# A hybrid decoder layer: dilated and MLA head pairs in turn, and six buffers for the copied-out value columns

## The chip, the cores and the metric

The kernel runs on one core of a Trainium2 chip, as one launch. The metric is the device time of that launch in microseconds, the median of the runs. TensorE (PE) does matrix products and transposes; its weight loads are listed apart (PEld). VectorE (DVE), ScalarE (ACT) and GpSimd (POOL) do elementwise work, and SyncE (SP) issues every DMA of this kernel from one queue that is worked off in order.

## The reference, cut to what matters

One causal decoder layer over 1024 tokens of width 1024, in float32. A combined input projection gives the latents of eight multi-head-latent (MLA) heads and the queries, keys and values of eight dilated heads. The two head groups are independent of each other; both results go into one output projection, then a gated feed-forward part with a short causal convolution follows.

```python
h = rms_norm(x, g_mix_norm[l]) * (1.0 + sc1[:, None]) + sh1[:, None]
proj = h @ w_in[l]
q_lat, kv_lat, k_pe, qd, kd, vd = jnp.split(proj, SPLITS, axis=-1)
...
o_mla = causal_dense_attention(q_mla, k_mla, v_mla, (MLA_NOPE + MLA_ROPE) ** -0.5)
...
o_dil = dilated_attention(qd, kd, vd)
mix = jnp.concatenate([o_mla.reshape(B, S, MLA_HEADS * MLA_V),
                       o_dil.reshape(B, S, DIL_WIDTH)], axis=-1) @ w_o[l]
x = x + g1[:, None] * mix
```

The dilated attention is a weighted sum of three banded softmaxes; the kernel computes it as one masked softmax whose mask holds the logarithm of how many bands a key lies in.

## The kernel before, in words

Every float32 product is made of float32r parts: an operand is split into a rounded part (`hi`, copied by ACT) and a rest (`lo`, subtracted by DVE or POOL), and two or three products are accumulated in PSUM.

The work comes in stages. First the input projection: after the latents, a loop over `u` in (0, 1) takes 256 columns each of the dilated queries, the dilated keys (both through `rope_chunk`, L350) and the dilated values (L466 to L471). Each of these makes eight token tiles `p` of 24 products on PE. The query and key tiles pass ACT, DVE and POOL (norm and rotation) and are written to DRAM (`qd_s`, `kd_s`, L369). A value tile is only copied from PSUM by ACT into `vo` (L470) and written to `vd_s` (L471). Four PSUM banks hold `p`. Between the chunks `ada_late` works off columns of `w_ada` on DVE; these weights and those of the projections share three `raw` buffers.

Then the latents are transposed (L491) and split by ACT and DVE (L492, L493), and two more projections give the MLA queries, keys and values, which are written to DRAM as well. They begin with `ql_hi`, and their weights pass `split_weights` (L91 on ACT, L97 on POOL).

Then the attention, one pair of heads after another. `sources` lists the pairs: 0 to 3 are dilated, 4 to 7 MLA. `attention_loads` (L501) brings queries, keys and values of a pair from DRAM, into one buffer each (`ql_t`, `kl_t`, `vl_t`). `prepared` (L532) transposes and splits them into tiles tagged `qk`, of which there are eight. An MLA pair takes all eight: `hi` and `lo` of queries and keys for two heads. A dilated pair takes four, and then builds stacked operands by 12 DMA copies of 64 partitions by 1024 floats (L554), 0.26 MB each: `q2` and `k2` have one buffer per head, and the two `k3` are the fifth and sixth `qk` tile. A score of a dilated pair is two products over 128 rows, that of an MLA pair three over 96. Pair 0 is prepared without copies, from tiles of its own.

For a pair, `scores` (L627) runs for the first four query tiles (`hf` 0) of both heads and then for the last four (`hf` 1): products, mask and row minimum on DVE (L641), exponential on ACT (L644), normalization on POOL (L645, L646). `weighted_values` (L660) transposes the weights and multiplies them with the split values. It is called one half late: the last half of a pair comes after the first scores of the next. `prepared` for the next pair is called after the `hf` 1 scores of a pair, and the loads of the pair after that at the end of the loop body. The load of the keys of the last pair is `first_load`: the loads of the output projection's weights (L790, L791) are queued behind it on SP.

The order of the instructions on each engine is not the program's: a scheduler works it out from the program's order as priority and from its own model of the times, and gives a tile a buffer when one is free in that model. At run time each engine takes its instructions in that order.

Of the kernel before, what the change touches and what calls it, by code (L numbers as in the profile page):

```python
# [8 lines left out]
F32 = mybir.dt.float32  # L9
# [9 lines left out]
P = 128  # L19
# [22 lines left out]
def hybrid_layer(ctx, tc, x, c, positions, w_ada, b_ada, g_mix_norm, w_in, g_q_lat, w_q_b, g_kv_lat, w_kv_b,  # L42
# [183 lines left out]
    def scale_cols(gm, j, base, g0):  # L226
        V.scalar_tensor_tensor(gm[:, 2 * j:2 * j + 2], in0=modc[:, base + 2 * j:base + 2 * j + 2], scalar=1.0,
                               in1=cols[:, g0 + 2 * j:g0 + 2 * j + 2], op0=ALU.add, op1=ALU.mult)
# [30 lines left out]
    def proj_weights(c0, n):  # L259
        raw = raw_tile(KD, n)  # L260
        nc.sync.dma_start(raw, w_in[:, c0:c0 + n].rearrange("(k p) n -> p k n", p=P))
        return split_weights(raw, KD, n)
# [5 lines left out]
    def proj_mm(w, t, n):  # L268
        ps = bank("p")
        for k in range(KD):  # L270
            proj_step(ps, w, t, n, k)
        return ps
# [59 lines left out]
    ap = phA.enter_context(tc.tile_pool(name="phAw", bufs=1, reuse_waits="tile"))  # L332
# [14 lines left out]
    def ada_late(j, row_form=False):  # L347
        ada_chunk(j, ada_load(j, raw_tile(KD, 256)), row_form, True)

    def rope_chunk(c0, tabc, tabs, dst, col):  # L350
        w = proj_weights(c0, 256)
        for t in range(NT):
            ps = proj_mm(w, t, 256)
            p3 = ps[:, 0:256].rearrange("p (h d) -> p h d", d=HD)
            b3 = [P, 4, HD]
            xn = ap.tile(b3, F32, tag="xn", name="xn", bufs=4)
            A.activation(xn, p3, AF.Copy)
            sq = ap.tile(b3, F32, tag="sq", name="sq", bufs=2)
            A.activation(sq, xn, AF.Square)
            ss = ap.tile([P, 4], F32, tag="ss", name="ss", bufs=4)  # L360
            V.tensor_reduce(ss, sq, op=ALU.add, axis=AX.X)
            r = rstd_of(ap, ss, 4, 1.0 / HD, "h4")
            V.tensor_tensor(xn, xn, r[:, :, None].to_broadcast(b3), op=ALU.mult)
            o = ap.tile(b3, F32, tag="ro", name="ro", bufs=4)
            G.tensor_tensor(o, xn, tabc[:, t:t + 1, :].to_broadcast(b3), op=ALU.mult)
            b = ap.tile(b3, F32, tag="rb", name="rb", bufs=3)
            swap_mult(V, b, xn, tabs[:, t, :], 0, HD)
            V.tensor_tensor(o, o, b, op=ALU.add)
            nc.sync.dma_start(dst[t, :, col:col + 256], o)  # L369
# [89 lines left out]
    for u in range(2):  # L459
        rope_chunk(C_QD + u * 256, qc, qs, qd_s, u * 256)  # L460
        ada_late(16 + 2 * u)
        ada_late(12 + 2 * u)
        rope_chunk(C_KD + u * 256, kc, ks, kd_s, u * 256)
        ada_late(17 + 2 * u)
        ada_late(13 + 2 * u)
        w = proj_weights(C_VD + u * 256, 256)  # L466
        for t in range(NT):
            ps = proj_mm(w, t, 256)
            o = ap.tile([P, 256], F32, tag="vo", name="vo", bufs=2)
            A.activation(o, ps[:, 0:256], AF.Copy)  # L470
            nc.sync.dma_start(vd_s[t, :, u * 256:(u + 1) * 256], o)  # L471
        for j in range(2):
            scale_cols(gm2, 2 * u + j, 32, G0_FFN)
            ada_late(20 + 2 * u + j)
# [26 lines left out]
    def attention_loads(q_s, k_s, v_s, pr, wd):  # L501
        ql = bl.tile([P, NT, 2 * wd], F32, tag="ql", name="ql_t", bufs=1)
        nc.sync.dma_start(ql, q_s[:, :, pr * 2 * wd:(pr + 1) * 2 * wd].rearrange("t p c -> p t c"))
        kl = bl.tile([P, NT, 2 * wd], F32, tag="kl", name="kl_t", bufs=1)
        kins = nc.sync.dma_start(kl, k_s[:, :, pr * 2 * wd:(pr + 1) * 2 * wd].rearrange("t p c -> p t c"))
        vl = bl.tile([P, NT, P], F32, tag="vl", name="vl_t", bufs=1)
        nc.sync.dma_start(vl, v_s[:, :, pr * P:(pr + 1) * P].rearrange("t p c -> p t c"))
        return ql, kl, vl, kins.ins

    def transposed(loads, wd, hh, fused, first=False):  # L510
        tag = "x"
        gain = 1.0 if fused else kgc[0:MW, 0:1]
        rows_ = 2 * wd if fused else wd
        pair = []
        for src, tg, g in ((loads[0], "q", 1.0), (loads[1], "k", gain)):
            if first:
                hi, lo = [bl.tile([P, S], F32R, tag=f"{tg}2{u}", name=tg + "2", bufs=1) for u in range(2)]
            else:
                hi, lo = [ap.tile([P, S], F32R, tag="qk", name=tg + u, bufs=8) for u in ("hi", "lo")]
            for hf in range(2):  # L520
                ps = bank(tag)
                for i in range(4):
                    T.transpose(ps[0:rows_, i * P:(i + 1) * P], src[:, 4 * hf + i, hh * wd:hh * wd + rows_], ident)
                cs = slice(hf * 512, hf * 512 + 512)
                A.activation(hi[0:rows_, cs], ps[0:rows_, :], AF.Copy, scale=g)
                V.scalar_tensor_tensor(lo[0:rows_, cs], in0=ps[0:rows_, :], scalar=g,
                                       in1=hi[0:rows_, cs].bitcast(F32), op0=ALU.mult, op1=ALU.subtract)
            pair.append((hi, lo))
        return pair

    sources = [(qd_s, kd_s, vd_s, pr, HD) for pr in range(4)] + [(qm_s, km_s, vm_s, pr, MW) for pr in range(4)]
    def prepared(pr, loads):  # L532
        if pr >= 4:
            heads = []
            for hh in range(2):
                (qh, ql), (kh, kl) = transposed(loads, MW, hh, False)
                heads.append([(a[0:MW, :], b[0:MW, :]) for a, b in ((qh, kh), (qh, kl), (ql, kh))])
            return heads
        (qh, ql), (kh, kl) = transposed(loads, HD, 0, True, pr == 0)
        heads = []  # L540
        if pr == 0:
            for odd in range(2):
                me = slice(64 * odd, 64 * odd + 64)
                heads.append([(a[me, :], b[me, :]) for a, b in ((qh, kh), (qh, kl), (ql, kh))])
            return heads
        for odd in range(2):
            me = slice(64 * odd, 64 * odd + 64)
            other = slice(64 - 64 * odd, 128 - 64 * odd)
            q2 = bl.tile([P, S], F32R, tag=f"q2{odd}", name="q2", bufs=1)
            k2 = bl.tile([P, S], F32R, tag=f"k2{odd}", name="k2", bufs=1)  # L550
            k3 = ap.tile([P, S], F32R, tag="qk", name="k3", bufs=8)
            for dst, rows_, src in ((q2, me, qh), (q2, other, ql), (k2, me, kh), (k2, other, kh),
                                    (k3, me, kl), (k3, other, kl)):
                nc.sync.dma_start(dst[rows_, :].bitcast(F32), src[me, :].bitcast(F32))  # L554
            heads.append([(q2, k2), (q2, k3)])
        return heads

    loaded = attention_loads(qd_s, kd_s, vd_s, 0, HD)
    for u in range(2):
# [3 lines left out]
        for t in range(NT):  # L563
# [14 lines left out]
            o = mp.tile(b3, F32, tag="ro", name="rom", bufs=4)  # L578
# [11 lines left out]
    for u in range(2):  # L590
# [3 lines left out]
        for t in range(NT):  # L594
# [6 lines left out]
            vo = mp.tile([P, 4, VD], F32, tag="vo", name="vom", bufs=3)  # L601
# [7 lines left out]
            o = mp.tile([P, 4, MW], F32, tag="ro", name="rok", bufs=4)  # L609
# [13 lines left out]
    ap = phB.enter_context(tc.tile_pool(name="phB", bufs=1, reuse_waits="tile"))  # L623
# [36 lines left out]
    def weighted_values(hf, prs, vs, mrow):  # L660
# [21 lines left out]
        for odd, po in enumerate(pos):  # L682
# [2 lines left out]
            A.activation(half[me, :], po[64:128, :], AF.Copy)  # L685
            V.tensor_tensor(mix[me, mrow, hf * 512:hf * 512 + 512], po[0:64, :], half[me, :], op=ALU.add)

    pending = None
    nxt = attention_loads(*sources[1])
    for pr in range(8):  # L690
        mask = masks[:, 1 if pr < 4 else 0, :]
        vl = split_values(loaded[2])
        for hf in range(2):
            ps_ = [scores(hf, terms, mask) for terms in tq]
            if hf == 1 and pr < 7:
                loaded = nxt
                tq_next = prepared(pr + 1, loaded)
            if pending is not None:
                weighted_values(*pending)
            pending = (hf, ps_, vl, pr)  # L700
        if pr < 7:
            tq = tq_next
            if pr < 6:
                nxt = attention_loads(*sources[pr + 2])
                first_load = nxt[3]
    weighted_values(*pending)
    phB.close()
# [232 lines left out]
```

## Time and profile before

| | us |
|---|---|
| time before, median of 3 runs (1502.28 to 1513.4) | 1502.96 |
| the profiled execution, time | 1514.05 |
| the profiled execution, span from first to last instruction | 1512.0 |
| PE busy in the span | 1424.9 (94%) |
| DVE busy | 853.4 (56%) |
| POOL busy | 657.2 (43%) |
| ACT busy | 595.7 (39%) |

The profiled execution is 11.1 us above the median of the runs. Times within the trace are us from the start of its span. A busy PE is not PE at its peak, since its instructions overlap and its clock is granted at one of two levels, 1.2 and 2.4 GHz; the granted clock of a stretch is given as a share of the higher.

### The profile page before, as it was taken

The page shows a single profiled execution, that of the slowest core. Times are in us where ns is not written, and L with a number is a line of the kernel's source. Part 1 is how long each engine was busy: PE and PEld are TensorE (multiplying, and loading weights), DVE is VectorE, ACT ScalarE, POOL GpSimd, SP SyncE. Part 2 cuts the span into 40 slices and gives each one's busy share as a digit, 9 for nine tenths or more (in the row PEclk, how much of TensorE's full clock was granted, in tenths as well). Part 3 has the DMA queues.
Part 4 walks back from the last instruction along what each step waited for, and adds up shares of the span by engine and source line. Part 5 has one row for each costly group of instructions (what it writes and reads, how often), then busy time and mean ns, then how long its engine had stood idle before and what let it go on. Part 6 is the DMA issues. An engine that isn't in the chain of part 4 may idle for free.

```text
span 1512.0 us, 21542 instructions
## 1 busy us (share of the span) xinstructions
PE 1424.9 (94%) x8021; PEld 1232.0 (81%) x8021; DVE 853.4 (56%) x1785; ACT 595.7 (39%) x1118; POOL 657.2 (43%) x680
## 2 busy tenths in 40 slices
PE   6899989799878999999999999999999999999998
PEld 4889989686666887879998888888888888888887
DVE  4577968587467988876654342433424344342444
ACT  4434223286467888864434312221221222122120
POOL 3355736367455766734653332332333133233330
PEclk9999989998689999999999999999999999999999
DMA  9544364537256212003330111101101111111102
GB/s 328 184 127 130 116 197 128 157 106 226 60 126 140 57 56 84 29 5 122 126 118 25 54 56 56 56 28 57 56 28 57 56 56 53 32 56 47 60 6 111
DMA packets 121711, 134.99 MB, mean 89 GB/s; under 512 B 5762, under 2 KB 112648, under 8 KB 121480
## 3 DMA queue, kind: packets, MB, share of 16 engines
q1 hardware_dynamic: 121608, 133.64, 28.5%
q8 instruction: 63, 1.03, 0.3%
q14 instruction: 40, 0.33, 0.1%
HBM read 105.30 MB, written 18.87 MB: 82 GB/s over the span
## 4 chain that ended last, share of the span: by engine, by line
PE 69%; DVE 4%; DMA 3%; ACT 2%; POOL 2%; issue 1%; SPq 1%; DVEq 0%; ACTq 0%; POOLq 0%
PE wide L103 11%; PE wide L104 11%; PE wide L102 11%; PE d L104 5%; PE d L102 5%; PE d L103 5%; PE s L639 4%; PE o L680 4%; PE x L669 4%; PE bank L104 1%; PE bank L103 1%; PE bank L102 1%; PE p L102 1%; PE p L103 1%; DMA k<-khi 1%
## 5 line engine op out<-in xcount | busy, mean ns | idle before, releaser
L97 POOL TENSOR_TENSOR w_lo<-raw,w_hi 128x512 fp32r<-128x512 f32 (+2 forms) x162 | 224.5, 1417 | 334.9 <-ACT w_hi L91 334.8
L102 PE MATMUL wide<-h,w_hi 128*128 128x512 f32 x704 | 273.8, 389 | 0.7 <-ACT junkE L809 0.7
L103 PE MATMUL wide<-h,w_hi 128*128 128x512 f32 x704 | 274.0, 389 | 0.0
L104 PE MATMUL wide<-h,w_lo 128*128 128x512 f32 x704 | 274.0, 389 | 0.0
L882 DVE TENSOR_TENSOR x<-d,x 128x512 f32<-128x512 f32 x176 | 118.3, 687 | 167.8 <-PE d L104 167.7
L91 ACT ACTIVATE w_hi<-raw 128x2048 fp32r<-128x2048 f32 (+3 forms) x54 | 101.0, 1870 | 246.9 <-PE wide L103 138.8
L841 DVE SCALAR_TENSOR_TENSOR y<-wide,ccols,y 128x1023 f32<-128x1023 f32 x44 | 56.2, 1280 | 244.8 <-ACT y L840 244.8
L102 PE MATMUL p<-w_hi,h_hi 128*128 128x256 f32 (+1 forms) x576 | 167.1, 291 | 10.1 <-ACT vo L470 9.6
L103 PE MATMUL p<-w_lo,h_hi 128*128 128x256 f32 (+1 forms) x576 | 164.7, 287 | 0.0
L104 PE MATMUL p<-w_hi,h_lo 128*128 128x256 f32 (+1 forms) x576 | 161.6, 287 | 0.6 <-DVE h_lo L257 0.5
L102 PEld LDWEIGHTS wide<-h,w_hi 128*128 128x128 f32 x704 | 132.0, 188 | 28.3 <-ACT junkE L809 0.8
L103 PEld LDWEIGHTS wide<-h,w_hi 128*128 128x128 f32 x704 | 132.2, 188 | 27.6 <-DVE h L767 0.2
L104 PEld LDWEIGHTS wide<-h,w_lo 128*128 128x128 f32 x704 | 132.1, 188 | 27.3
L864 POOL TENSOR_TENSOR m_lo<-y,m_hi 128x1024 fp32r<-128x1024 f32 x22 | 52.7, 2396 | 205.9 <-ACT m_hi L863 205.9
L103 PE MATMUL d<-w_lo,m_hi 128*128 128x512 f32 x352 | 136.9, 389 | 0.0
L104 PE MATMUL d<-w_hi,m_lo 128*128 128x512 f32 x352 | 136.9, 389 | 0.0
L102 PE MATMUL d<-w_hi,m_hi 128*128 128x512 f32 x352 | 132.5, 389 | 0.0
L102 PEld LDWEIGHTS p<-w_hi,h_hi 128*128 128x128 f32 x576 | 112.6, 196 | 11.1 <-ACT vo L470 10.1
L645 POOL TENSOR_TENSOR st<-st,negone 128x1 f32<-128x1 f32 x128 | 70.0, 551 | 102.6 <-ACT pt L644 86.3
L103 PEld LDWEIGHTS p<-w_lo,h_hi 128*128 128x128 f32 x576 | 112.7, 196 | 0.1
L104 PEld LDWEIGHTS p<-w_hi,h_lo 128*128 128x128 f32 x576 | 109.8, 193 | 1.1 <-DVE h_lo L257 1.0
L676 DVE TENSOR_TENSOR pT_lo<-x,pT_hi 128x512 fp32r<-128x512 f32 (+1 forms) x160 | 97.5, 632 | 21.1 <-ACT pT_hi L675 17.1
(245 smaller groups left out, 3061.6 us busy)
## 6 DMA issues: line engine op xcount, KB each, us to landing
raw<-in_w_up_dram SPq DMA_DIRECT2D x22, 1024.0 KB, 5.1
raw<-in_w_ada_dram SPq DMA_DIRECT2D x16, 1024.0 KB, 8.1
raw<-in_w_down_dram SPq DMA_DIRECT2D x11, 1024.0 KB, 4.8
ada<-in_w_ada_dram SPq DMA_DIRECT2D x8, 1024.0 KB, 5.2
raw<-in_w_in_dram SPq DMA_DIRECT2D x8, 1024.0 KB
raw<-in_w_o_dram SPq DMA_DIRECT2D x16, 512.0 KB, 5.3
xr<-in_x_dram SPq DMA_DIRECT2D x32, 128.0 KB, 3.7
out_dram<-x SPq DMA_DIRECT2D x16, 256.0 KB, 2.0
```

Source lines behind the costliest of these rows:

```text
L91: A.activation(hi, raw, AF.Copy)
L97: G.tensor_tensor(lo[:, i:i + 2, :], raw[:, i:i + 2, :], hi[:, i:i + 2, :].bitcast(F32), op=ALU.subtract)
L102: T.matmul(ps, lhsT=a[0], rhs=b[0], start=first, stop=False)
L103: T.matmul(ps, lhsT=a[0], rhs=b[1], start=False, stop=False)
L104: T.matmul(ps, lhsT=a[1], rhs=b[0], start=False, stop=last)
L639: T.matmul(ps[:, 0:b - a], lhsT=q_[:, qs_], rhs=k_[:, a:b], start=(m == 0), stop=(m == len(terms) - 1))
L645: G.tensor_tensor(st[:, 3:4], st[:, 2:3], negone, op=ALU.pow)
L669: T.transpose(px[:, c0 + (i - i0) * P:c0 + (i - i0 + 1) * P], pr[i][:, kj * P:(kj + 1) * P], ident)
L676: V.tensor_tensor(lo[:, 0:c0], px[:, 0:c0], hi[:, 0:c0].bitcast(F32), op=ALU.subtract)
L680: T.matmul(pos[odd][:, i0 * P:], lhsT=vs[:, kj, odd, :, :], rhs=part[:, b0:b0 + n], start=(kj == 0 and part is hi), stop=(kj == last and p ...
L841: V.scalar_tensor_tensor(y[:, 1:], in0=ps[:, 0:S - 1], scalar=ccols[:, 88 + ch:89 + ch], in1=y[:, 1:], op0=ALU.mult, op1=ALU.add)
L882: V.tensor_tensor(x1s[t][:, cs], ps, x1s[t][:, cs], op=ALU.add)
```

## The change

The pairs are taken in the order 0, 4, 1, 5, 2, 6, 3, 7 instead of 0 to 7, and what was counted by `pr` (the next pair to prepare, the pair to load) is counted by the place in that order. The rows of `mix` that a pair writes and the mask that it uses stay its own. The copied-out value tiles `vo` of the input projection have six buffers of 1 KB per partition instead of two.

```diff
-            o = ap.tile([P, 256], F32, tag="vo", name="vo", bufs=2)
+            o = ap.tile([P, 256], F32, tag="vo", name="vo", bufs=6)
             A.activation(o, ps[:, 0:256], AF.Copy)
             nc.sync.dma_start(vd_s[t, :, u * 256:(u + 1) * 256], o)
...
+    ORDER = (0, 4, 1, 5, 2, 6, 3, 7)
     pending = None
-    nxt = attention_loads(*sources[1])
-    for pr in range(8):
+    nxt = attention_loads(*sources[ORDER[1]])
+    for n, pr in enumerate(ORDER):
         mask = masks[:, 1 if pr < 4 else 0, :]
         vl = split_values(loaded[2])
         for hf in range(2):
             ps_ = [scores(hf, terms, mask) for terms in tq]
-            if hf == 1 and pr < 7:
+            if hf == 1 and n < 7:
                 loaded = nxt
-                tq_next = prepared(pr + 1, loaded)
+                tq_next = prepared(ORDER[n + 1], loaded)
             if pending is not None:
                 weighted_values(*pending)
             pending = (hf, ps_, vl, pr)
-        if pr < 7:
+        if n < 7:
             tq = tq_next
-            if pr < 6:
-                nxt = attention_loads(*sources[pr + 2])
+            if n < 6:
+                nxt = attention_loads(*sources[ORDER[n + 2]])
                 first_load = nxt[3]
     weighted_values(*pending)
```

## Rows read from the trace of the kernel before

**Rows 1.** Busy time by stretch: us, PE, PEld, DVE, ACT, POOL, granted clock, DMA share, GB/s.

```profile
core 0: us, PE busy (x) PEld busy (x) DVE busy (x) ACT busy (x) POOL busy (x), PEclk, DMA share, GB/s
800.00:1000.00 200.00, 200.00 (x888) 165.48 (x887) 78.78 (x81) 53.47 (x43) 66.53 (x40) 1.00 0.13 43
```

**Rows 2.** Who PE waited for: us in total, times, longest.

```profile
PE s L639 <- DMA k<-khi: 18.7, 4, 7.6
PE p L102 <- ACT vo L470: 9.6, 3, 4.3
PE p L102 <- ACT ql_hi L492: 7.7, 1, 7.7
...
PE s L639 <- DMA k<-klo: 0.9, 1, 0.9
```

**Rows 3.** PE in order of time: start, duration, instruction, idle time before it.

```profile
193.98 0.39 PE L102 MATMUL p<-w_hi,h_hi 128*128 128x256 f32 x1 [2.27 <-ACT vo L470]
...
206.37 0.58 PE L102 MATMUL p<-w_hi,h_hi 128*128 128x256 f32 x1 [4.27 <-ACT vo L470]
...
281.40 0.28 PE L104 MATMUL p<-w_hi,h_lo 128*128 128x256 f32 x1
...
291.50 0.69 PE L102 MATMUL p<-w_hi,ql_hi 128*128 128x384 f32 x1 [7.66 <-ACT ql_hi L492]
```

**Rows 4.** ACT and SP in order of time, the value chunks.

```profile
193.54 0.38 ACT L470 ACTIVATE vo<-p 128x256 f32<-128x256 f32 x1 [12.59 <-DMA vd_s<-vo]
...
289.39 1.47 ACT L91 ACTIVATE w_hi<-raw 128x1536 fp32r<-128x1536 f32 x1
...
175.96 15.60 SPq L369 DMA_DIRECT2D kd_s<-ro  x5
...
276.96 0.38 SPq L561 DMA_DIRECT2D raw<-in_w_q_b_dram  x1
```

**Rows 5.** Busy time by stretch, three stretches behind PE's waits in the projection.

```profile
195.00:199.00 4.00, 4.00 (x23) 4.00 (x22) 2.84 (x7) 0.00 (x0) 0.84 (x1) 0.57 1.08 358
206.00:215.00 9.00, 8.63 (x50) 8.63 (x51) 5.19 (x11) 4.07 (x7) 3.97 (x4) 0.64 0.18 58
...
290.00:295.00 5.00, 3.50 (x14) 3.41 (x15) 2.07 (x3) 2.64 (x5) 3.62 (x2) 0.56 0.92 294
```

**Rows 6.** SP's queue where pairs 2 and 3 are prepared.

```profile
427.04 0.36 SPq L503 DMA_DIRECT2D ql_t<-qd_s  x1
...
467.43 0.36 SPq L503 DMA_DIRECT2D ql_t<-qm_s  x1
...
474.93 2.23 SPq L554 DMA_DIRECT2D k<-klo  x2
```

**Rows 7.** PE in order of time: the first scores of pairs 2 and 3.

```profile
442.83 1.09 PE L639 MATMUL s<-k,q 128*128 128x128 f32 x3 [7.59 <-DMA k<-khi]
...
481.92 1.09 PE L639 MATMUL s<-k,q 128*128 128x128 f32 x3 [4.68 <-DMA k<-khi]
```

**Rows 8.** Busy time by stretch around the preparations of pairs 1 to 3, and later.

```profile
467.00:490.00 23.00, 15.64 (x89) 12.48 (x87) 14.82 (x40) 16.00 (x35) 14.63 (x20) 0.85 0.98 228
...
443.00:450.00 7.00, 7.00 (x35) 6.41 (x35) 2.95 (x11) 2.94 (x9) 1.47 (x3) 0.64 0.96 184
482.00:490.00 8.00, 7.14 (x41) 6.62 (x41) 3.77 (x12) 4.59 (x12) 3.03 (x6) 0.78 1.05 229
405.00:418.00 13.00, 12.38 (x53) 9.96 (x54) 7.98 (x23) 8.64 (x23) 7.88 (x16) 0.66 0.28 60
...
590.00:600.00 10.00, 7.36 (x51) 6.78 (x50) 8.07 (x20) 7.49 (x17) 6.69 (x10) 0.91 0.44 135
```

**Rows 9.** PE and SP where one MLA pair follows another (pairs 5 and 7 prepared).

```profile
540.61 0.60 PE L523 MATMUL x<-ident,ql_t 128*96 128x128 f32 x4
...
547.42 0.36 SPq L507 DMA_DIRECT2D vl_t<-vm_s  x1
...
587.07 0.58 SPq L790 DMA_DIRECT2D raw<-in_w_o_dram  x1
```

**Rows 10.** One of the three products of an MLA score: duration in ns, min/median/max.

```profile
L639 PE MATMUL s<-khi,qlo x96: 274/339/522, 512.3 to 662.1; 96*128 96x384 f32 x24, 96*128 96x512 f32 x24, 96*128 96x320 f32 x16, 96*128 96x448 f32 x16
```

## The prediction

> **What bounds the kernel now.** I read the busy time by stretch first, then the list of what PE waited for, then the order of time around the long waits. In the feed-forward part PE is busy all the time at the full clock [rows 1], and nothing there depends on when it begins; so time that PE wins earlier moves the end forward by as much. The list of PE's waits [rows 2] shows where it can win: 19.6 us on the copies of `k` in the attention (18.7 + 0.9), 9.6 us on ACT's `vo`, and 7.7 us on `ql_hi`. The reader should see that the two edits aim at the first two lines, and that the third hangs on the second: ACT takes its instructions in order, and `ql_hi` stands behind the last `vo` and a weight split [rows 4].
>
> **Edit one, six buffers for `vo`.** It removes waits and adds no instruction: 16 copies and 16 stores remain, and 4 KB per partition more are used. With two buffers the third copy of the first value chunk waits 12.59 us [rows 4] for a store that has not been issued, since SP stands until 191.56 in stores of the rotated keys, which wait for DVE [rows 4]. Behind that copy on ACT are the other copies; their `p` banks stay full, and PE stops for 2.27 and 4.27 us [rows 3], in the second chunk for the remaining 9.6 - 6.5 = 3.1 us. With six buffers the seventh copy is the first that can wait. The second copy ended at 193.54 - 12.59 = 180.95; a chunk of eight tiles takes at most 25 us later on (281.40 - 206.37 = 75.0 us for three chunks, 3.1 us of waiting and a slow spell included [rows 3]), so a tile is due every 3 us or less and the seventh copy near 195. The first store had landed by 193.54 [rows 4]. So I cost the remaining wait at nothing; if SP were held longer by more than the 1.5 us between, it would come back one for one.
>
> After the waits the clock is low: 0.57 over 4.00 us, 0.64 over 8.63 us busy, 0.56 over 3.50 us [rows 5]. Taken as work lost, that is 4.00 x 0.43 + 8.63 x 0.36 + 3.50 x 0.44 = 6.4 us. Together the edit can give at most 9.6 + 7.7 + 6.4 = 23.7 us, and at least nothing, if something else is late at the same place.
>
> What is late next? The second value chunk would end some 15 us earlier than its 281.40 [rows 3]: 9.6 of waits and 4.9 of the first two slow spells. Then `ql_hi` must follow. On ACT a weight split (1.47 us at 289.39) stands before it, and the load for that split is issued at 276.96 [rows 4], when DVE has given a `raw` buffer free. That load depends on DVE's work on `w_ada`, not on `vo`, and DVE comes forward only as far as PE feeds it. I bound what remains of the 7.7 us between 3 us (three to four evacuations have to be made before the next product) and 7.7, with the slow spell of 1.5 us on top, and a little for DVE: I take 8.7 us of the 23.7 as kept. The edit gives 15 us, between 6 and 20.
>
> **Edit two, the order.** It moves work and adds none. It moves the preparations of pairs 1 to 6, with their loads and with 36 copies (12 for each of pairs 1, 2, 3), to other places in SP's queue.
>
> What it removes: three changes from a dilated pair to a dilated pair. Each ends in a wait for copies, 19.6 us in all [rows 2]. Why they wait is in the order of time: from the load of `ql_t` to the first scores of the prepared pair it takes 442.83 - 427.04 = 15.8 us for pair 2 and 481.92 - 467.43 = 14.5 us for pair 3 [rows 6, 7], and over 467 to 490 the DMA engines are at 0.98 and move 228 GB/s [rows 8]. Twelve copies of 0.26 MB and two loads of 0.79 MB are 4.7 MB, which at 228 GB/s is 20.7 us. So it is the amount that takes the time, not the issue. PE arrives at the scores at 435.2 and 477.2 (start less wait [rows 7]), 8.2 and 9.8 us behind the load, and stands, since it takes its order as it is: the scheduler put the scores there.
>
> What it adds: three changes from an MLA pair to a dilated pair (4 to 1, 5 to 2, 6 to 3), with the same 12 copies and the MLA loads of the pair after. Do the copies start earlier there? `q2` and `k2` are then free long before. But an MLA pair holds all eight `qk` tiles until its `hf` 1 scores of the first head are done, and the dilated pair's transposes are split into those tiles. In the change from MLA to MLA the first transposes end at about 541.2 (540.61 + 0.60) [rows 9], and such a start is what the copies have to wait for too. So the lock moves from `q2` to `qk`, and the copies start about as late against the scores as before. The cover on PE is a little longer: the second head's `hf` 1 scores have eight more products, of 0.339 us each by the row [rows 10], or 2.7 us; as products overlap I take 1.5. Per change the wait is then 14.5 - 9.8 - 1.5 = 3.2 by pair 3 and 15.8 - 8.2 - 1.5 = 6.1 by pair 2; I take the mean, 4.7, and 0.7 for the second head's copies (0.9 of rows 2 is one such wait): 5.4 us.
>
> The change 6 to 3 has one thing more. The output weights follow `first_load` on SP at once: at 587.07 [rows 9] they are issued in the change from 5 to 6, when no copies are there. In the new order `first_load` comes while pair 3 is prepared, and the 1.05 MB of weights go ahead of most of its copies: 4.6 us at 228 GB/s. So the three waits are 5.4 + 5.4 + 10.0 = 20.8 us against 19.6. Bounds: 3 x 3.2 = 9.6 us and 3 x 6.8 + 4.6 = 25 us.
>
> The changes from dilated to MLA (four instead of one) need no copies; a dilated pair leaves six `qk` tiles free, and I cost them at nothing, hidden by the dilated pair's own scores; if that cover fails it is under 1 us each. In turn the weights no longer disturb MLA pairs as they do from 590 to 600, where PE idles 2.6 us [rows 8]; they do it within a wait that is counted: 2 us won. The slow spells behind the waits (0.66 over 13 us, 0.64 over 7, 0.78 over 8 [rows 8], in lost time 4.4 + 2.5 + 1.8 = 8.7 us) stay, since there are three waits of about the same length as before. The edit gives -1.2 + 2 = 0.8 us, say 1.
>
> **The Trainium skill on this.** The copies and the MLA work load different parts of the chip: DMA is at 0.98 in one stretch and PE and the others are busy in the other [rows 8]. The Trainium skill's page Perfetto Trace Analysis, section Optimization Strategy, says that where a kernel has several regimes with different contended engines, interleaving those regimes may help; by that rule the order would win what the second rival below says. The trace speaks against it so far: the copies lie at the seam between two pairs, and the seams with copies stay three. The Trainium skill's page DMA: Bandwidth & Descriptors, section Rules for kernel authors, says that two transfers to disjoint halves of the partitions share the same engines and gain nothing over one; the 228 GB/s at a share of 0.98 agree with that, so copies that are issued together would not land sooner.
>
> **The sum.** 15 + 1 = 16 us: 1514.05 - 16 = 1498 for the profiled execution. That one is 11.1 us above the median of the runs; where these 11 us lie I cannot tell from one trace, so I take the same 16 us from the median: 1503 - 16 = 1487.
>
> **The rivals.**
> First, `vo`'s wait is followed by another at the same place: DVE's `w_ada` work and the `raw` buffers set the load at 276.96, and ACT stands in the weight split instead of in `vo`. For it: that load comes only 4.4 us before PE's last value product. Against it: PE's three waits name `vo`. Then the edit gives 6 us and the order 1: 1496.
> Second, alternation hides the copies: `q2` and `k2` free early lets the scheduler put values work of the MLA pair before the dilated scores. Then the 19.6 us and the 8.7 us of slow clock go: 1503 - 15 - 28 = 1460. For it: work for PE is there (the MLA pair's last half). Against it: the eight `qk` tiles, and that the scheduler has put the scores too early three times out of three.
> Third, slower: at the MLA pair's end SP issues the load of `vl_t` first, at 547.42, when POOL has split the values, and what follows in the queue waits; the first transposes were through at 541.2 [rows 9]. If in the new order the loads and copies stand behind that load, each of the three waits is 6.2 us longer: 20.8 + 18.6 = 39.4 us against 19.6. With 2 us more of slow clock the order costs 22 us less the 2 of the weights, and with 15 won the time is 1503 + 20 - 15 = 1508. It decides from the point where the seam's wait passes 12 us: then the whole kernel is slower than before. Against it: where dilated pairs are prepared, `ql_t` goes first and `vl_t` last.
> That the edits don't do what they say (the six buffers in use, the order followed) I see no way for.
>
> **How the numbers follow.** A measurement here tells about 1% (15 us) from no change, so 1488 and 1518 are the borders. Forecast 0.47 (1478 to 1497 by its bounds; slightly more than half of it under 1488), first rival 0.2, second 0.15, third 0.13, and 0.05 for a schedule that changes elsewhere, to either side. The range leaves out the far part of the second rival and little else: 1464 to 1508. Faster 0.25 + 0.15 + 0.03 + 0.02 = 0.45; slower by over 1% is only the far end of the third rival and of the rest, 0.07; same 0.48.
>
> **What would show it.** PE's list of waits without `vo`, and ACT without the 12.59 us; the first product of the MLA projections near 275 instead of 291.50. Three waits of PE on `k` copies remain, at the seams 4 to 1, 5 to 2 and 6 to 3, about 5, 5 and 10 us, each with a low clock behind it; none at the seam behind pair 0. The second rival shows as the absence of these waits, the third as `vl_t` ahead of the copies on SP and waits above 10 us. I am wrong if the waits at the seams leave the list, or if ACT's wait before `ql_hi` only changes its name.

## The result, and the profile after

The changed kernel takes 1488.7 us (median of 21 runs, 1480.7 to 1510.85) against 1511.7 us for the kernel before, measured beside it (21 runs, 1502.28 to 1517.54): a ratio of 0.9842, with an interval of 0.9822 to 0.9863. Measured once more beside the last experiments it took 1503.68 us against 1508.23, a ratio of 0.9926 (0.9887 to 0.9966). To read both numbers one needs to know that the 33 runs of the changed kernel form two groups, 17 with a mean clock above 0.975 and a median of 1486.7 us, and 16 below it with 1504.9 us, and that the ratios leave out the ten runs of the second group that lie over 1.5% above the fastest; by the means of all runs they are 0.989 and 0.994. In which stage the groups part is shown below; what starts it stays open. The profiled execution is one of the second group: 1502.14 us, span 1500.4, to be set beside the 1514.05 and 1512.0 of before.

The list of what PE waited for, after, answers to [rows 2] (in us: total, times, longest):

```profile
PE s L639 <- DMA k<-khi: 14.5, 3, 5.5
...
PE x L523 <- ACT vs L656: 3.8, 1, 3.8
...
PE p L102 <- ACT xn L357: 3.4, 1, 3.4
...
PE p L102 <- ACT ql_hi L492: 2.2, 1, 2.2
```

`vo` has left the list. In its place stands a shorter wait that the list of before doesn't have: 3.4 us on `xn`, at 245.70, ahead of the second value chunk, where ACT itself has waited 4.82 us for POOL's `ro`. The copies of `k` are still its first line, with three waits where there were four.

ACT and SP in order of time around the value chunks, against [rows 4]:

```profile
192.51 0.38 ACT L470 ACTIVATE vo<-p 128x256 f32<-128x256 f32 x1 [2.44 <-PE p L104]
195.38 0.38 ACT L470 ACTIVATE vo<-p 128x256 f32<-128x256 f32 x1 [2.49 <-PE p L104]
...
276.12 1.48 ACT L91 ACTIVATE w_hi<-raw 128x1536 fp32r<-128x1536 f32 x1 [1.82 <-DMA raw<-in_w_q_b_dram]
...
172.47 19.84 SPq L369 DMA_DIRECT2D kd_s<-ro  x7
192.40 1.10 SPq L471 DMA_DIRECT2D vd_s<-vo  x2
...
271.30 0.38 SPq L561 DMA_DIRECT2D raw<-in_w_q_b_dram  x1
```

SP still stands until 192.31 (172.47 + 19.84) in the stores of the keys, and the first two `vo` are stored only then. But ACT now waits for PE's products (2.44 us each time) and not for a store. The copy at 195.38 is the seventh of the chunk, the first that needs a buffer back.

PE in order of time: the first product of the MLA projection [rows 3], the start of the attention (the transposes of pair 4), and the first scores of pairs 1, 2 and 3:

```profile
278.23 0.44 PE L102 MATMUL p<-w_hi,ql_hi 128*128 128x384 f32 x1 [2.25 <-ACT ql_hi L492]
...
349.42 1.92 PE L523 MATMUL x<-ident,ql_t 128*96 128x128 f32 x8 [3.82 <-ACT vs L656]
...
432.06 1.11 PE L639 MATMUL s<-k,q 128*128 128x128 f32 x3 [5.54 <-DMA k<-khi]
...
506.25 1.09 PE L639 MATMUL s<-k,q 128*128 128x128 f32 x3 [4.48 <-DMA k<-khi]
...
583.22 0.64 PE L639 MATMUL s<-k,q 128*128 128x128 f32 x3 [4.51 <-DMA k<-khi]
```

The MLA projection starts at 278.23 instead of 291.50, 13.3 us earlier. From there to the end of the span it takes 1500.4 - 278.23 = 1222.2 us, before 1512.0 - 291.50 = 1220.5. So in these two executions all of the gain lies ahead of the MLA projection, and the new order of the pairs has given nothing. The busy time by stretch says why, first before (the stage of pair 0, which [rows 8] don't hold), then after:

```profile
370.00:380.00 10.00, 9.34 (x30) 6.22 (x30) 5.36 (x17) 5.54 (x13) 10.00 (x16) 0.65 0.77 188
380.00:390.00 10.00, 10.00 (x33) 7.51 (x32) 5.47 (x15) 4.47 (x10) 4.18 (x6) 0.50 0.00 0
390.00:400.00 10.00, 8.98 (x33) 6.57 (x32) 4.76 (x11) 4.97 (x9) 3.03 (x4) 0.66 0.14 27
```

```profile
350.00:390.00 40.00, 40.00 (x127) 27.42 (x125) 20.12 (x58) 21.23 (x47) 22.49 (x34) 0.50 0.22 63
390.00:400.00 10.00, 10.00 (x45) 8.18 (x45) 6.16 (x20) 6.16 (x16) 5.13 (x9) 0.70 0.00 1
400.00:410.00 10.00, 10.00 (x65) 8.78 (x64) 8.49 (x20) 8.11 (x18) 6.31 (x13) 1.00 0.00 0
...
430.00:440.00 10.00, 7.95 (x43) 7.71 (x43) 3.37 (x11) 3.86 (x8) 0.00 (x0) 0.66 0.97 198
500.00:510.00 10.00, 5.23 (x25) 4.69 (x24) 2.23 (x5) 2.42 (x6) 2.94 (x4) 0.76 1.07 245
580.00:590.00 10.00, 6.66 (x35) 6.01 (x36) 4.86 (x13) 4.78 (x12) 1.33 (x3) 0.83 1.08 246
```

After, PE has no idle time from 350 to 390 and yet works at the lower of its two clock levels throughout; that is 40.00 x 0.50 + 10.00 x 0.30 = 23 us of work lost by 400. Before, the three rows shown lose 9.34 x 0.35 + 5.0 + 8.98 x 0.34 = 11.3 us. The seams give some of it back: the waits on `k` are 14.5 us instead of 19.6, and the clock behind them loses 7.95 x 0.34 + 5.23 x 0.24 + 6.66 x 0.17 = 5.1 us instead of 8.7. Not all of that is the order's: with the buffers alone the waits on `k` are 15.7 us already (below).

### The profile page after: what moved, and what is told of

It is laid out like the page before. It is cut to its first block, busy times and chain, and to the rows that moved or that the text cites. A ratio compares the mean times of both kernels' runs of the same rounds, so it can differ in the third digit from the quotient of the medians.

```text
span 1500.4 us, 21545 instructions
## 1 busy us (share of the span) xinstructions
PE 1427.1 (95%) x8021; PEld 1233.2 (82%) x8021; DVE 853.5 (57%) x1785; ACT 594.9 (40%) x1118; POOL 655.3 (44%) x680
## 4 chain that ended last, share of the span: by engine, by line
PE 69%; DMA 4%; DVE 3%; ACT 2%; issue 2%; POOL 2%; SPq 0%; DVEq 0%; POOLq 0%; ACTq 0%
PE wide L103 11%; PE wide L104 11%; PE wide L102 11%; PE s L639 6%; PE d L102 5%; PE d L103 5%; PE d L104 5%; PE o L680 5%; PE x L669 4%; DMA k<-khi 2%; DMA raw<-in_w_o_dram 2%; POOL w_lo L97 1%; PE x L523 1%; PE p L102 1%; PE p L103 1%
## 5 line engine op out<-in xcount | busy, mean ns | idle before, releaser
L645 POOL TENSOR_TENSOR st<-st,negone 128x1 f32<-128x1 f32 x128 | 73.6, 581 | 107.0 <-ACT pt L644 105.2
```

The source lines that it names most:

```text
L645: G.tensor_tensor(st[:, 3:4], st[:, 2:3], negone, op=ALU.pow)
```

## The experiments

My theory was that the buffers give nearly all of the gain by starting the MLA projection earlier, and that the order only moves the waits on the copies. The rivals: the alternation hides the copies, or another wait steps in for `vo`.

**The buffers alone, and the order alone.**

```diff
 e1_vo6:   vo bufs=2 -> 6, pairs in the order 0 to 7
 e2_order: vo bufs=2, pairs in the order 0, 4, 1, 5, 2, 6, 3, 7
```

> Six buffers for vo, pairs in the old order 0 to 7. My theory: this edit alone gives about 15 of the 16 us of the forecast; in the trace the first product of the MLA projections comes near 277 us, as in the changed kernel, instead of 291.5, PE's list of waits has no vo, and the waits on k copies at the seams 0 to 1, 1 to 2 and 2 to 3 stay at about 19 us. Ratio to the kernel before 0.985 to 0.993. The rival that the order is what wins expects less than 0.5% here.

> The new order of the pairs, two buffers for vo. My theory: nothing measurable, 0 to 5 us won, with PE's three waits on vo (9.6 us) and the 7.7 us before ql_hi still there, and three waits on k copies of about 5 us each at the seams 4 to 1, 5 to 2 and 6 to 3. Ratio 0.996 to 1.001. The rival that alternation hides the copies expects 1% or more here and no waits on k copies.

The buffers alone: 1497.76 us (7 runs, 1491.61 to 1500.86) against 1511.35, ratio 0.9909 (0.9876 to 0.9941); their waits on the copies are 15.7 us, and not the 19 that I expected. The order alone: 1510.16 us (12 runs), ratio 1.0012 (0.9972 to 1.0052); its runs fall in two groups as those of the changed kernel do, six from 1501.11 to 1505.68 us and six from 1514.65 to 1524.06. PE's first product of the MLA projection, with the buffers alone and then with the order alone:

```profile
279.87 0.44 PE L102 MATMUL p<-w_hi,ql_hi 128*128 128x384 f32 x1 [3.26 <-ACT ql_hi L492]
```

```profile
291.47 0.60 PE L102 MATMUL p<-w_hi,ql_hi 128*128 128x384 f32 x1 [4.62 <-ACT ql_hi L492]
```

The earlier start goes with the buffers and not with the order. The order alone keeps PE's waits for `vo` and for the copies:

```profile
PE s L639 <- DMA k<-khi: 14.0, 2, 7.5
PE p L102 <- ACT vo L470: 10.3, 3, 4.1
PE s L639 <- DMA k<-klo: 5.9, 1, 5.9
```

14.0 + 5.9 = 19.9 us on copies against the 19.6 of [rows 2]: hidden they are not.

**Four buffers instead of six.**

```diff
-            o = ap.tile([P, 256], F32, tag="vo", name="vo", bufs=6)
+            o = ap.tile([P, 256], F32, tag="vo", name="vo", bufs=4)
```

> The changed kernel with 4 buffers instead of 6 for the copied-out value columns. Theory A, what must be bridged is one stay of the issuing queue of about 20 us in which one column tile comes every 2.9 us beside it only from 9 us on: four buffers are filled by then, the wait of ScalarE is at most 2 us and the MLA projection starts within 2 us of the changed kernel's 277.5 us. Rival, each buffer is worth its share of the 13 us: two buffers fewer give back about half, and the stage starts near 284 us.

One run: 1510.32 us, span 1508.5. My theory missed, and as far as one run tells the rival came out: the MLA projection starts at 284.83, about halfway between 291.50 and 278.23. ACT, and below it SP, in order of time show where:

```profile
194.64 0.39 ACT L470 ACTIVATE vo<-p 128x256 f32<-128x256 f32 x1 [7.05 <-DMA vd_s<-vo]
...
205.60 0.38 ACT L470 ACTIVATE vo<-p 128x256 f32<-128x256 f32 x1 [10.01 <-DMA vd_s<-vo]
...
196.31 1.28 SPq L198 DMA_DIRECT2D raw<-in_w_ada_dram  x2
197.69 1.47 SPq L471 DMA_DIRECT2D vd_s<-vo  x1
```

I had counted on the queue's first stay alone. When SP is free again at 192.67, two stores go out, then loads of weights stand ahead of the third (197.69), and the copy after those waits another 10.01 us.

**What holds the copies at the seams.** In the first run the second head's copies are queued behind the first head's; in the second, where an MLA pair precedes a dilated one, the loads of the pair after next, and so the output weights, are queued behind the last copy.

Here `copied` is the list of the copies issued so far.

```diff
 e3_by_head:
...
+            with (tc.issue_after(copied[-1]) if odd else ExitStack()):
                 for dst, rows_, src in ((q2, me, qh), (q2, other, ql), (k2, me, kh), (k2, other, kh),
 e4_loads_behind:
-                nxt = attention_loads(*sources[ORDER[n + 2]])
+                with (tc.issue_after(copied[-1]) if ORDER[n + 1] < 4 else ExitStack()):
+                    nxt = attention_loads(*sources[ORDER[n + 2]])
```

> The changed kernel with the six copies of the second head of a dilated pair queued on SP behind the six of the first head. My theory of the seam: PE waits for an amount of data. In the changed kernel ten of the twelve copies stand ahead of the last one that the first scores need; here six do, 1.05 MB less, at some 230 GB/s 4.6 us less. So the three waits of PE of 4.5 to 5.5 us shrink to about 1 us each or go, and the second head's scores may wait up to 4 us instead. 0 to 12 us under the changed kernel. If the wait is one of latency behind the last split (klo), and not of amount, the waits stay as they are.

> The changed kernel with the loads of the pair after next queued behind the last copy at the seams from MLA to dilated, and with them the output weights at the seam 6 to 3. It takes 1.57 MB of queries and keys, and 1.05 MB of weights at one seam, out of the way of the copies. By amount: 6.9 us less ahead of the first scores at 228 GB/s, so the three waits of 4.5 to 5.5 us go, and the time is 10 to 20 us under the changed kernel (the low clock behind the waits goes too). If the copies' own issue and splits set the wait, it shrinks by under 2 us each.

Neither changes the time beyond what the two groups of runs allow: 1501.37 us (9 runs, 1484.18 to 1504.4; 0.9907, 0.987 to 0.9944) and 1501.57 us (4 runs, 1480.63 to 1507.41; 0.9898, 0.9832 to 0.9963). PE's waits on copies, of the first and then of the second:

```profile
PE s L642 <- DMA k<-khi: 12.3, 2, 8.5
...
PE s L642 <- DMA k<-klo: 2.2, 2, 1.7
```

```profile
PE s L641 <- DMA k<-khi: 5.7, 2, 3.0
...
PE s L641 <- DMA k<-klo: 1.9, 3, 0.9
```

Sorting the copies by head gives nothing (14.5 us again, and one seam's 3.78 us that the trace puts to no engine). With the loads behind them it is 7.6 us, and 2.82 us more at one seam without a named cause. In five profiles with the seams of the changed kernel (two of that kernel, two with 128 rows and one with wider buffers, below) the waits are 14.0 to 16.8 us, so the loads in the queue make up a quarter to a half of them. What makes up the rest isn't shown. Both expectations were missed: the waits did not go, and where 6.9 us of transfers were to be out of the way at each seam, the wait fell by 1.4 to 2.3 us per seam, measured from the changed kernel's 14.5 for the three. So the amount of data alone does not set it.

**No copies at all.** Pairs 1 to 3 are prepared as pair 0 is, and scored with three products over 64 rows per tile of scores, in place of two over 128.

```diff
-        (qh, ql), (kh, kl) = transposed(loads, HD, 0, True, pr == 0)
+        (qh, ql), (kh, kl) = transposed(loads, HD, 0, True, True)
         heads = []
-        if pr == 0:
+        if pr < 4:
```

> The changed kernel, but the dilated pairs 1 to 3 are prepared as pair 0 is: no copies between row halves, and three score products over 64 rows in place of two over 128. Theory A, the three waits at the seams are the copies' and nothing else: no wait of over 1 us at the starts of pairs 1, 2 and 3 (14.5 us less with 2 to 4 us of clock), against 24 products more in each pair of 0.36 us (26 us): about 10 us slower than the changed kernel if the clock stays at 1.00 through 64-row products. Theory B, 64-row products keep TensorE at its lower clock: windows at 0.50 through the stages of pairs 1 to 3, 72 products of each at 0.57 instead of 0.29 us, so 50 to 70 us slower. Rival, the wait is the transposes' and not the copies': waits of 3 us or more stay at the seams.

1495.96 us (8 runs), ratio 0.9929 (0.9889 to 0.9969): 9 us above the changed kernel's first group, as theory A had it. No wait of over 0.5 us stands ahead of a score, so the waits at the seams came with the copies. The edit also takes the tiles of pairs 1 to 3 out of the eight `qk` tiles, so it doesn't tell the copies themselves from the wait for the tiles that they start from. Theory B, that 64-row products always run at the lower clock, is wrong for the stage of pair 1 and yet not without ground in that of pair 2:

```profile
420.00:450.00 30.00, 29.58 (x167) 21.78 (x166) 24.52 (x58) 22.66 (x43) 14.55 (x20) 1.00 0.14 41
...
475.00:480.00 5.00, 5.00 (x32) 4.40 (x31) 4.91 (x13) 4.90 (x11) 4.27 (x5) 1.00 0.71 193
480.00:485.00 5.00, 4.38 (x22) 3.00 (x21) 4.94 (x15) 5.00 (x11) 4.70 (x7) 0.89 0.77 229
485.00:490.00 5.00, 5.00 (x14) 3.09 (x14) 0.40 (x1) 1.36 (x5) 3.02 (x6) 0.50 0.00 0
...
500.00:505.00 5.00, 5.00 (x19) 3.93 (x18) 1.46 (x4) 1.79 (x3) 1.24 (x2) 0.50 0.00 0
505.00:510.00 5.00, 5.00 (x26) 4.24 (x24) 2.08 (x4) 1.79 (x3) 0.00 (x0) 0.72 0.00 0
```

The first of pair 2's 64-row products starts at 480.66, and by 485 the clock is at 0.50; PE's only idle time between is 0.62 us ahead of a product at 481.83. The clock stays there while PE is busy all the time, and is back at 1.00 from 510 on, though products over 64 rows run until 529.

**Why pair 0's stage is slow.** The first edit gives pair 0's products all 128 rows, for both heads; the second widens the buffers whose wait holds up the start of the attention.

```diff
 e5_rows128, and e12_rows128_again:
-                me = slice(64 * odd, 64 * odd + 64)
-                heads.append([(a[me, :], b[me, :]) for a, b in ((qh, kh), (qh, kl), (ql, kh))])
+                heads.append([(a, b) for a, b in ((qh, kh), (qh, kl), (ql, kh))])
 e6_vom8:
-            vo = mp.tile([P, 4, VD], F32, tag="vo", name="vom", bufs=3)
+            vo = mp.tile([P, 4, VD], F32, tag="vo", name="vom", bufs=8)
```

> The changed kernel, but pair 0's score products read all 128 rows of its transposed tiles instead of 64 per head, so that both heads of pair 0 get the sum of their scores (its part of the output is changed); the count, the columns and the order of the instructions stay. Theory A, the products over 64 rows keep TensorE at the lower of its two clock levels through pair 0's stage: in every run the clock is back at 1.00 within some 10 us of the first score product, no run at a mean clock under 0.975, all runs at 1480 to 1490 us. Theory B, the gap of 3.8 us ahead of the stage lowers the clock, and it stays down by chance whatever the products read: the runs still fall in two groups, at about 1485 and 1504 us, as the changed kernel's do, and the profile may show 0.50 from 350 to 390 us. Rival C, the rows don't matter and the split is of the chip and not of this stage: the windows of pair 0's stage show 1.00 and the runs still split.

> The run with pair 0's products over all 128 rows once more (both heads of pair 0 get the sum of their scores, so its part of the output is changed), since six runs of it say little: of the changed kernel's 33 runs 17 had a mean clock over 0.975. Theory A, the products over 64 rows are what lets the clock stay down: every run at 1480 to 1491 us again. Theory B, chance: about half of the runs at 1500 us or more.

> The changed kernel with 8 buffers instead of 3 for the copied-out value columns of the MLA value projection; the program's order of instructions around pair 0's first scores moves a little with it. Theory A, the wait of 2.77 us of ScalarE for a store of these columns is what holds the attention's first value split, and TensorE's 3.8 us behind it: the ScalarE wait is gone, the gap before the first transpose of pair 4 is at most 2.0 us, the clock drops less at the start, median 2 to 4 us below the changed kernel's, more runs in the faster group. Rival, the loads of pair 4 end the wait as well: the ScalarE wait goes and TensorE's gap stays within 1 us of 3.8 us; no change in the time.

With 128 rows all twelve runs of the two measurements lie between 1480.58 and 1486.77 us (medians 1483.15 and 1484.14, ratios 0.9818, 0.9783 to 0.9853, and 0.9821, 0.9788 to 0.9853). If rows didn't matter, twelve of the first group in a row would have a chance of (17/33)^12 = 0.0003, or 0.003 by the 13 of 21 of the first measurement. The version with the wider buffers, which keeps 64 rows and ran beside the first six, has two of six runs in the second group. The same stretch of time with 128 rows, and below it with the wider buffers and 64 rows:

```profile
350.00:360.00 10.00, 9.73 (x57) 8.66 (x56) 7.55 (x26) 9.22 (x23) 8.70 (x16) 0.83 0.44 137
360.00:370.00 10.00, 9.95 (x61) 8.35 (x60) 9.97 (x27) 9.13 (x20) 9.80 (x14) 1.00 0.39 115
370.00:380.00 10.00, 10.00 (x67) 9.15 (x67) 9.10 (x32) 9.31 (x24) 9.48 (x16) 1.00 0.01 2
```

```profile
350.00:360.00 10.00, 10.00 (x38) 6.85 (x36) 7.39 (x21) 9.33 (x25) 9.70 (x16) 0.50 0.36 108
360.00:370.00 10.00, 10.00 (x31) 6.83 (x30) 5.46 (x14) 4.14 (x10) 4.64 (x9) 0.50 0.36 105
370.00:380.00 10.00, 10.00 (x29) 6.42 (x27) 3.93 (x11) 3.29 (x7) 4.57 (x6) 0.50 0.00 0
```

With the wider buffers ACT's wait for a store is gone and the gap ahead of pair 4's transposes falls from 3.82 to 2.26 us, but the clock is low all the same in the profile, and the time is 1489.98 us (6 runs, 1484.69 to 1504.93; 0.9859, 0.981 to 0.9909), in two groups again. Pair 0's products read 64 rows in the run with the loads behind the copies too, and its profiled execution lies with the first group (1480.63 us, mean clock 0.984):

```profile
350.00:360.00 10.00, 8.97 (x52) 6.72 (x53) 7.25 (x25) 8.36 (x22) 8.28 (x15) 0.84 0.37 118
360.00:370.00 10.00, 9.95 (x51) 6.73 (x50) 9.50 (x26) 8.20 (x18) 9.71 (x14) 1.00 0.45 134
370.00:380.00 10.00, 10.00 (x56) 7.45 (x55) 7.07 (x22) 7.44 (x18) 6.77 (x10) 1.00 0.01 2
```

So the groups part in this stage, and 64 rows let the clock stay down without forcing it. The gap ahead of pair 4's transposes is 3.63 us there, and 3.70 in the second profile of the changed kernel, whose clock is at 0.50 from 350 to 390: the size of that gap isn't what decides. No profile of the changed kernel itself in its first group was taken.

**Towards a faster version.** Pair 0 gets stacked operands too, by copies during the MLA projection, and per tile of scores one product over 128 rows and one over 64; the second version adds the two edits named in its expectation. The changed kernel ran beside them once more, without an edit.

```diff
 e9_pair0, in prepared, pr == 0:
...
+                q2, k2 = [bl.tile([P, S], F32R, tag=f"{c}{odd}", name=c, bufs=1) for c in ("q2", "k2")]
+                for dst, rows_, src in ((q2, me, qh), (q2, other, ql), (k2, me, kh), (k2, other, kh)):
+                    nc.sync.dma_start(dst[rows_, :].bitcast(F32), src[me, :].bitcast(F32))
+                heads.append([(q2, k2), (q2[me, :], kl[me, :])])
...
 e10_all: e9_pair0, with e4_loads_behind's edit, and vom bufs=3 -> 4
```

> The changed kernel itself once more, beside the two versions built on it. Every theory: 1480 to 1511 us in two groups, at about 1485 us with a mean clock of 0.98 and at about 1505 us with 0.967, median in either.

> The changed kernel with pair 0 prepared much as the other dilated pairs: eight copies between row halves during the MLA projection, and then per tile of scores one product over 128 rows and one over 64 in place of three over 64 (24 products of 0.36 us fewer at the full clock); for the room, the weighted values get one buffer less for the upper part, and the halves share a buffer with the lower part. Theory A, the products over 64 rows are what lets the clock stay at its lower level after the gap at the start of the attention: the windows from 360 us show 1.00, no run at a mean clock under 0.975, and 5 to 9 us less than the changed kernel's faster runs: 1476 to 1482 us in all of them. Theory B, the clock stays down by chance whatever the products read: two groups again, each some 8 us below the changed kernel's. Rival, the copies come too late, or the two buffers are missed in the weighted values: a wait of several us ahead of the first score product or of the value products, and no gain.

> The version before with two edits more: the loads of the pair after next behind the last copy at the three seams (as in the run with the loads behind, whose three waits were 8.5 us in place of 14.5), and 4 instead of 3 buffers for the copied-out MLA value columns. Theory A: waits of 8 to 10 us in all at the seams, no wait of ScalarE for a store at the start of the attention, 4 to 7 us below the version before: 1470 to 1478 us. Rival: the pairs' loads come later and their transposes wait for them, which gives the gain back; within 2 us of the version before.

The changed kernel's two groups came again (four runs of twelve in the first). Pair 0 with copies is slower, 1515.42 us (12 runs), 1.003 (1.0002 to 1.0059): no gain, as its rival had it, though with other waits. Its profile has the gap ahead of pair 4's transposes at 5.93 us and the waits on `khi` at 19.7, and with one of two products still over 64 rows the clock is low from 360 to 390:

```profile
PE s L644 <- DMA k<-khi: 19.7, 3, 7.9
...
PE x L524 <- ACT vs L661: 5.9, 1, 5.9
```

With both edits more it is 1487.49 us (6 runs, 1485.11 to 1490.49), 0.9867 (0.9833 to 0.9902). The waits on copies are 8.0 us there, with 3.04 us more at one seam without a named cause, and the clock is at 1.00 from 360 on with the same products in pair 0's stage. The 1470 to 1478 that I expected are missed, by 9.5 us at the median and 7.1 at the lowest run. It is steadier than the changed kernel and not shown to be faster: its interval overlaps with both of that kernel's, and its median lies at that of the first group.

## Why the prediction was right

**The time, 1487 forecast and 1488.7 measured: met, in part by luck.** The 16 us were taken from 1503, the median of three runs; beside the changed kernel the one before took 1511.7. So the gain was 23.0 us in the first measurement and 4.6 in the second (1508.23 - 1503.68), as the median falls into one group or the other.

**The buffers, costed at 15 us: right.** Alone they gave 1511.35 - 1497.76 = 13.6 us, and the MLA projection starts 291.50 - 279.87 = 11.6 us earlier in their profile, 13.3 in that of the changed kernel. That the seventh copy would be the first to need a buffer, near 195, came as worked out (195.38), and nobody waits there. Of the 23.7 us that were at stake I had taken 8.7 as kept; about 10 were. That part was sized by a guess between bounds and not by its pieces: of the 7.66 us ahead of the projection 2.25 remain, below my lower bound of 3, and ACT has waited 1.82 us ahead of them for the weights' load that the first rival named. So the mechanism of that rival exists, at 1.8 us and not at its price of 9. A larger piece I had not looked for: the 3.39 us on `xn`, with a clock of 0.93 over the 21.61 us busy from 240 to 265, or 1.5 us of work lost. 2.25 + 3.39 + 1.5 = 7.1 of the 10; the rest I can't place. Nor had I seen how little slack six buffers leave: with four, half of the earlier start is lost in the one run made.

**The order, costed at 1 us won: not contradicted in the sum, with one term mis-sized and one missing.** Alone its median is 1.2 us less, and its ratio of 1.0012 has an interval of about 4 us less to 8 more; 1 us can't be told from nothing. The seams 4 to 1 and 5 to 2, forecast at 5.4 us each, took 5.54 and 4.48, and 5.26 and 7.04 in the second profile of the changed kernel. The seam 6 to 3, forecast at 10.0, took 4.51 in both: the 4.6 us for the output weights ahead of the copies were too much. SP in order of time at that seam:

```profile
565.46 0.36 SPq L503 DMA_DIRECT2D ql_t<-qm_s  x1
...
570.84 0.63 SPq L505 DMA_DIRECT2D kl_t<-km_s  x1
571.52 1.40 SPq L791 DMA_DIRECT2D raw<-in_w_o_dram  x1
572.97 2.05 SPq L554 DMA_DIRECT2D k<-khi  x3
...
581.75 0.87 SPq L507 DMA_DIRECT2D vl_t<-vm_s  x1
582.99 1.23 SPq L792 DMA_DIRECT2D raw<-in_w_o_dram  x1
```

One of the two loads of a column stretch goes ahead of the copies of `k`, 0.5 MB and not 1.05, the other stands behind them. From the load of `ql_t` to the first score it takes 583.22 - 565.46 = 17.8 us, so PE, which stands for 4.51 of them, also came later than I had it. The working by amount was wrong too: its 20.7 us don't fit into the 14.5 to 15.8 us that they were to explain, and with less data ahead the waits fell by less than it says. That the eight `qk` tiles hold the copies back I read from the program; no run gave them more buffers. The 2 us for the output weights were not measured apart. The missing term is pair 0's stage: I looked at the clock behind waits only and took a busy PE to be one that recovers. That the two errors nearly cancel is luck of the executions: in a run of the second group the stage of pair 0 takes what the seams gave, in one of the first the changed kernel lies about 11 us below the buffers alone (1486.7 against 1497.76), which sets the better half of one kernel's runs beside all seven of the other's. What the order adds to the buffers isn't shown.

**The rivals.** The second is refuted: three waits on the copies stay, and with the order alone they are as long as before. By the page Perfetto Trace Analysis of the Trainium skill, section Optimization Strategy, interleaving regimes may help; here it had a ratio of 1.0012 (0.9972 to 1.0052), and the copies stayed at the seams. The third is refuted by the same rows of SP: `ql_t` goes first and `vl_t` last. Of the changes from dilated to MLA, costed at nothing and under 1 us each if their cover failed, two show more: at the first the gap of 2.03 us of the buffers alone is 3.82, where ACT waits for a store, much as it had for `vo`; while pair 7 is prepared PE waits 2.03 us for DVE, at 610.77.

## What to carry to other kernels

Before adding buffers for a tile that is copied out, look at what stands ahead of its store in the issuing queue, and count how many tiles come in the whole of that stay and in the loads behind it: four buffers of six gave half here, not nearly all. Taking two kinds of work in turn did not hide the transfers here: ask first what a transfer waits for before it can be issued, and whether the new order brings that forward. When a kernel's times fall in two groups, compare the clock by stretch in a profile of either before a difference is put down to an edit.

## What the hardware showed that I had not expected

PE can be busy without a gap and stay at the lower clock: 40.00 us of 40.00 at 0.50 in pair 0's stage, where the products read 64 rows. With 128 rows in the same place the clock was back at 1.00 from 360 on, and all twelve runs lay in the first group. Products over 64 rows do not always run so: in pair 1's stage of the version without copies they ran at 1.00, and so they did from 360 on in pair 0's own stage in the profile of the run with the loads behind the copies. A product over 64 rows takes 0.57 us by the median at the lower level and 0.36 at the higher; 72 of them make 15 us of the 18 between the two groups of runs. The Trainium skill's page TensorE: Matmul & The Clock Gate, section What's actually happening, says that activity releases the throttle; the rows here agree for the 96- and 128-row products behind pair 0 (1.00 at 400) and for the 64-row products of that last profile (1.00 from 360 on), but not for those of the changed kernel's (0.50 over 40.00 us busy). What starts the fall in one run and not in another I could not settle: the gap ahead of the stage was made smaller and the groups stayed, and a gap of 3.6 to 3.8 us stood ahead of it in profiles of either group.
